# A planner of instruction order gets shared transfer queues, three transfer rates and a replay

## The chip, the cores and the metric

The kernel runs on one core of a Trainium2 chip. The time is device microseconds of one execution, median over runs. Before the change: 1165.82 us, median of 3 runs (1165.45 to 1168.76). The engines are TensorE (PE; its weight loads are listed as PEld), VectorE (DVE), ScalarE (ACT), GpSimd (POOL) and SyncE (SP, which here only issues transfers). Each engine works its own list of instructions strictly in the order in which they were issued; semaphores hold an instruction until its operands are there.

## The reference

A decoder trunk of two layers, 512 tokens, width 1024, float32. Cut to what matters:

```python
for layer in range(2):
    hn = rms_norm(h, attn_norm[layer])
    h = h + (swa_sink_mixer if layer == 0 else nsa_mixer)(hn, ...)
    h = h + swiglu(rms_norm(h, ffn_norm[layer]), w_gu[layer], w_down[layer])   # hidden width 2816
return rms_norm(h, final_norm)
```

Mixer A (layer 0) is attention over a window of 128 with sinks, 16 heads of 64 in 2 key groups. Mixer B (layer 1) adds compressed keys (a two-layer projection of blocks of 32 tokens), selected blocks and a window of 512, mixed by gates. Both have a shared table of relative biases.

## The kernel before

Activations lie transposed, as eight tiles of 128 features by 512 tokens. A float32 product is made of three passes in the format float32r: each operand is cut into a high half (`whi`, `xh`, ...) and the rest (`wlo`, `xl`, ...), and PE multiplies high by high, high by low and low by high.

Stages in order of time: the entry (loads of x, bias tables), the attention of mixer A, its output projection, the feed-forward of layer 0; then the entry of mixer B (key and value projections, compression: tiles `xf`, `xc`, `pc`), its attention, output projection, and the feed-forward of layer 1, which ends in `last_down` and the output.

**The feed-forward** uses `seven`: a product of 2 by 2 blocks in seven block products (`Z`, `X`, `Y` are its PSUM banks) instead of eight. For each of its calls SP loads two raw weight tiles (`raw`, three buffers), DVE makes the sums and differences `s`, ACT casts them to `whi`, DVE subtracts to get `wlo`. For two parts of each call (`wlo` of the first raw tile, and `w22l`) the low half is made by a transfer instead: ACT writes minus the rounded raw tile into it, and a transfer that POOL issues adds the source from HBM onto that, which leaves what the rounding lost (`halves_by_dma`). ACT also evacuates the first two partial sums of `Z` into `rv`, and PE can't start the next product into that bank before. There are 26 calls in each layer: 18 for the gate and up projections, 8 (`seven_down`) for the down projection in two groups of four.

**Buffers.** Most tiles of 128 by 512 come from one ring, `operand` (tag `op`, `NOP` = 38 buffers of 2 KB per partition). In a down stretch 8 of them hold `h`, 21 hold the forms of the hidden layer (7 for each of three blocks, function `hidden_forms`), and a `seven` call takes 4 (`s1`, `s2`, `w22h`, `w22l`), in the gate and up stretches 5 (with `rv`). `scratch` has another 6 (`NT`). `heads_out`, which ends an attention unit, copies half of a bank through a tile `ot` that has two buffers of its own.

**The order of all work** is not that of the source text. Every call of an engine is recorded as an `Op` with a price in ns, the ops that it depends on, and its tiles (class `Scheduler`, `add`); `issue` then lays out a plan and calls the ops in the plan's order. `plan` is a list scheduler: it goes through time, and each free engine takes the ready op with the smallest priority number if its tiles' buffers are free; the port that DVE and POOL share and ACT's table loads are in it. The first priorities come from the longest path to the end and the place in the source (`PLACE`); then `latest` runs the plan backwards and gives each op the latest start as its new priority. Six such rounds (`ROUNDS`) are made and the plan with the shortest own forecast is issued. A transfer in a plan waits for one single line that moves 358 bytes per ns; 1900 ns later it has landed, 1400 ns more for one that POOL issues. All instructions stand under line 119 of the profile, since one helper records them; tiles tell them apart.

Of the kernel before, what the change touches and what calls it, by code (L numbers as in the profile page):

```python
# [16 lines left out]
P = 128  # L17
# [20 lines left out]
RVB = 640  # L38
RVA = 384

NOP = 38
NT = 6
NPT = 2
NW = 3
# [9 lines left out]

PLACE = 300
ROUNDS = 6
DMA_LATENCY = 1900.0

WOK = 6

# [9 lines left out]

class Op:
    __slots__ = ("eng", "call", "cost", "preds", "after", "index", "span", "succs", "prio", "tiles", "table", "bytes", "port", "late")


class Scheduler:
# [46 lines left out]
    def add(self, name, m, call, writes, reads, args, kw):  # L122
        op = Op()
        op.eng, op.call, op.preds, op.succs, op.bytes, op.table, op.late = name, call, {}, [], 0, 0, 0.0
        op.prio = len(self.ops) + self.offset
        n = int(np.prod([c for _, c in writes[0].ap][1:]))
        psum = any("PSUM" in str(x.space) for x in writes + reads)
        parts = writes[0].ap[0][1]

        rows = sum(int(np.prod([c for _, c in x.ap][1:])) > 1 and "PSUM" not in str(x.space) for x in reads)  # L130
        op.port = rows > 0 if name == "pool" else name == "dve" and (
            rows > 1 or rows == 1 and not psum and m in ("tensor_scalar", "tensor_copy"))
        if name == "pe":
            f4 = 1 if m == "transpose" or "float32r" in str(reads[0].dtype) else 4
            op.cost = max(n * f4 * 0.449 + 4.5, 109.0)
        elif m == "dma_start" and name != "pool":
            op.bytes = 4 * int(np.prod([c for _, c in writes[0].ap]))
            op.cost = 475.0 if name == "sp" else 100.0
        elif name == "act":
            extra = sum(isinstance(kw.get(k), bass.AP) for k in ("bias", "scale", "accum_out"))  # L140
            op.cost = n * 0.83 + 93.0 * (1 + extra) - (40.0 if psum else 0.0) + (118.0 if parts == DH else 0.0)
            if m == "activation":
                op.table = self.TABLE.get(args[2].name, 0)
        elif name == "dve":
            if m == "reciprocal":
                op.cost = n * 6.2 + 65.0
            elif m == "memset" or (m in ("tensor_scalar", "tensor_copy") and not psum):
                op.cost = n * 0.52 + 130.0
            else:
                op.cost = n * 1.04 + 70.0 + (60.0 if m == "scalar_tensor_tensor" else 0.0) + (  # L150
                    110.0 if parts < P and n > 100 else 0.0) + (67.0 if m == "tensor_tensor_reduce" else 0.0)
        elif name == "pool":
            if m == "dma_start":

                op.bytes = 8 * int(np.prod([c for _, c in writes[0].ap]))
                op.cost, op.port, op.late = 1000.0, False, 1400.0
            elif m == "tensor_tensor":
                op.cost = n * 2.1 + 150.0
            else:
                op.cost = n * 0.83 + 162.0 + 82.0 * (len(args) > 2 and isinstance(args[2], bass.AP))  # L160
        op.tiles = {}
        for aps, write in ((writes, True), (reads, False)):
            for ap in aps:
                t, box = self.region(ap)
                past = self.seen.setdefault(t, ([], []))
                for w in (0, 1) if write else (0,):
                    for o, q in past[w]:
                        if o is not op and q[0] < box[1] and box[0] < q[1] and q[2] < box[3] and box[2] < q[3]:
                            op.preds[o] = True
                if t in self.tiles:  # L170
                    op.tiles[t] = True
        for aps, w in ((writes, 0), (reads, 1)):
            for ap in aps:
                t, box = self.region(ap)
                self.seen[t][w].append((op, box))
        self.ops.append(op)

    def issue(self):

        ops = self.ops  # L180
        for i, op in enumerate(ops):
            op.index = i
            op.span = op.cost + (op.bytes / 358.0 + DMA_LATENCY + op.late if op.bytes else 0.0)
            op.succs = []
        for op in ops:
            for p in op.preds:
                p.succs.append(op)
        for op in ops:
            op.after = [(q, self.lag(op, q)) for q in op.succs]
        far = {}  # L190
        for op in reversed(ops):
            far[op] = op.span + max((far[q] + (0.0 if q.eng == op.eng else 150.0) for q in op.succs), default=0.0)
        prio = [op.prio * PLACE - far[op] for op in ops]
# [12 lines left out]
    def latest(self, start, span, given):  # L206


        ops = self.ops
        free = {e: 0.0 for e in ("sp", "pe", "act", "dve", "pool")}  # L210
        using = {}
        for op in ops:
            for t in op.tiles:
# [13 lines left out]
        while n:  # L227
# [3 lines left out]
            for e in free:  # L231
# [14 lines left out]
                for p, lag in [(p, self.lag(p, op)) for p in op.preds] + [(p, 150.0) for p in before.get(i, ())]:  # L246
# [6 lines left out]
        return res  # L253

    def plan(self, prio):
        ops = self.ops
# [8 lines left out]
        free = dict(self.tags)  # L265
        first = {tag: 0 for tag in order}
        taken, end_of = set(), {}
        engines = ("sp", "pe", "act", "dve", "pool")
        busy = {e: 0.0 for e in engines}
        port = {"dve": 0.0, "pool": 0.0}  # L270
        ready = {e: [] for e in engines}
        soon = {e: [] for e in engines}
        events, releases = [0.0], []
        waiting = [len(op.preds) for op in ops]
        at = [0.0] * len(ops)
# [4 lines left out]
        table, dma, left, result = 0, 0.0, len(ops), []  # L280
        parked = {tag: [] for tag in order}
        early = {tag: 0 for tag in order}
        finish = 0.0
        freed, given = {tag: [] for tag in order}, {}

        def unpark(tag):
# [4 lines left out]
        def may_take(op):  # L291
# [21 lines left out]
                unpark(tag)  # L313
            return None

        while left:
            assert events, "no instruction can be issued"
            now = heapq.heappop(events)
            while events and events[0] <= now:
                heapq.heappop(events)  # L320
            while releases and releases[0][0] <= now:
                _, tag, t = heapq.heappop(releases)
                free[tag] += 1
                freed[tag].append(t)
                unpark(tag)
            again = True
            while again:
                again = False
                for e in engines:
# [23 lines left out]
                    if op.port:  # L353
                        port[e] = now + cost
                    if op.table and op.table != table:
                        table, cost = op.table, cost + 1280.0
                    start[i] = now
                    busy[e] = end = now + cost
# [3 lines left out]
                    finish = max(finish, end)  # L362
# [3 lines left out]
                    for t in op.tiles:  # L366
                        users[t] -= 1
                        end_of[t] = max(end_of.get(t, 0.0), end)
                        if not users[t]:
                            heapq.heappush(releases, (end_of[t] + 150.0, self.tiles[t], t))  # L370
                            heapq.heappush(events, end_of[t] + 150.0)
                    for q, lag in op.after:
                        k = q.index
                        at[k] = max(at[k], end + lag)
                        waiting[k] -= 1
                        if not waiting[k]:
                            heapq.heappush(soon[q.eng], (at[k], prio[k], k))
                            heapq.heappush(events, at[k])
        return finish, result, start, given


@with_exitstack
def trunk(ctx, tc, a, out):
# [1146 lines left out]
```

## Time and profile before

| | |
|---|---|
| median of 3 runs | 1165.82 us |
| profiled execution | 1163.0 us, its span 1161.2 us |
| granted clock, mean | 0.996 |
| PE busy | 1125.2 us, 97% of the span |
| DVE busy | 905.1 us, 78% |
| ACT busy | 753.4 us, 65% |
| POOL busy | 359.9 us, 31% |
| moved by transfers | 172.02 MB, 148 GB/s over the span |

A busy time is the time in which an engine had at least one instruction under way. "Idle before, releaser" tells how long an engine stood still before an instruction and whose result ended the wait. Transfers have queues: q0 is POOL's, q1 is SP's.

### The profile page before, as it was taken

How to read it: one execution, taken by the hardware profiler on the slowest of the kernel's cores; microseconds unless marked ns; L12 is line 12 of the kernel's file. 1: busy time of each engine (PE TensorE's matmuls, PEld its weight loads, DVE VectorE, ACT ScalarE, POOL GpSimd, SP SyncE). 2: the span in 40 equal slices, each digit the busy share in tenths (PEclk: the TensorE clock that was granted, in tenths of full speed). 3: DMA queues.
4: the chain of work that ended last, by engine and by line, in shares of the span. 5: the costliest groups of instructions: out<-in, count | busy, mean ns of one | idle time of the engine just before them, and what ended most of it. 6: DMA issues, size and time to landing. Idle time of an engine off the chain costs nothing. (4 is left out here: it accounts for less than half of the span.)

```text
span 1161.2 us, 20764 instructions
## 1 busy us (share of the span) xinstructions
PE 1125.2 (97%) x7347; PEld 1005.4 (87%) x7347; DVE 905.1 (78%) x2085; ACT 753.4 (65%) x1557; POOL 359.9 (31%) x519
## 2 busy tenths in 40 slices
PE   8999999999999999999899999999999999999997
PEld 6787787899999998987688788878879999999997
DVE  6999569478878886667788989857857898887764
ACT  5778279367657756552577888829637766775763
POOL 2467711011111121001466867771001121121101
PEclk9999999999999999999899999999999999999999
DMA  7845567477777786861454133156657868778832
GB/s 223 202 96 139 120 150 164 110 189 187 159 184 184 157 189 169 264 199 52 130 124 100 28 92 119 29 125 161 132 121 188 186 155 207 182 166 188 186 96 73
DMA packets 65072, 172.02 MB, mean 148 GB/s; under 512 B 7782, under 2 KB 15718, under 8 KB 64968
## 3 DMA queue, kind: packets, MB, share of 16 engines
q0 software_dynamic: 21312, 58.73, 30.5%
q1 hardware_dynamic: 43376, 111.81, 30.3%
q8 instruction: 58, 0.95, 0.3%
q14 instruction: 46, 0.38, 0.1%
q10 hardware_dynamic: 280, 0.16, 0.1%
HBM read 166.41 MB, written 4.26 MB: 147 GB/s over the span
## 5 line engine op out<-in xcount | busy, mean ns | idle before, releaser
L119 PE MATMUL Z<-xform,whi 128*128 128x256 f32 x864 | 165.0, 284 | 5.8 <-ACT rv L119 5.5
L119 ACT CAST whi<-s 128x512 fp32r<-128x512 f32 (+1 forms) x208 | 115.7, 585 | 76.0 <-PE X L119 47.6
L119 PE MATMUL X<-xform,whi 128*128 128x256 f32 x864 | 164.5, 281 | 0.0
L119 ACT CAST whi<-raw 128x1024 fp32r<-128x1024 f32 (+3 forms) x118 | 107.5, 915 | 71.6 <-PE O L119 27.6
L119 POOL DMA_DIRECT2D wlo<-in_ffn_gu x52 | 45.0, 865 | 339.5 <-ACT wlo L119 207.9
L119 DVE TENSOR_TENSOR wlo<-s,whi 128x512 fp32r<-128x512 f32 (+1 forms) x208 | 129.3, 646 | 17.3 <-ACT whi L119 14.9
L119 PEld LDWEIGHTS Z<-xform,whi 128*128 128x128 f32 x864 | 133.4, 189 | 8.8 <-ACT rv L119 7.0
L119 PEld LDWEIGHTS X<-xform,whi 128*128 128x128 f32 x864 | 135.1, 189 | 0.4
L119 PE MATMUL Z<-xform,wlo 128*128 128x256 f32 x432 | 121.8, 282 | 2.0 <-DMA wlo<-in_ffn_gu 2.0
L119 PE MATMUL X<-xform,wlo 128*128 128x256 f32 x432 | 119.8, 280 | 0.0
L119 DVE TENSOR_TENSOR s<-raw 128x512 f32<-128x512 f32 (+1 forms) x104 | 67.2, 646 | 27.6 <-DMA raw<-in_ffn_gu 22.3
L119 PE MATMUL S<-xh,whi 128*128 128x512 f32 (+1 forms) x216 | 85.7, 408 | 0.6 <-ACT whi L119 0.6
L119 PE MATMUL S<-xl,whi 128*128 128x512 f32 (+1 forms) x216 | 84.6, 405 | 0.0
L119 PEld LDWEIGHTS Z<-xform,wlo 128*128 128x128 f32 x432 | 81.8, 189 | 2.4 <-DMA wlo<-in_ffn_gu 2.4
L119 DVE TENSOR_TENSOR ptl<-PT,pth 128x512 fp32r<-128x512 f32 x108 | 72.5, 686 | 12.0 <-ACT pth L119 10.5
L119 PEld LDWEIGHTS X<-xform,wlo 128*128 128x128 f32 x432 | 81.2, 189 | 0.0
L119 ACT CAST pth<-PT 128x512 fp32r<-128x512 f32 x108 | 61.0, 582 | 30.9 <-PE PT L119 28.9
L119 PE MATMUL S<-xh,wlo 128*128 128x512 f32 x208 | 80.8, 403 | 0.0
L119 ACT ACTIVATE pb<-pb,nmb 128x128 f32<-128x128 f32 (+3 forms) x128 | 71.2, 559 | 9.8 <-DVE nmb L119 9.5
L119 POOL TENSOR_SCALAR pb<-pb,smb,gates 128x128 f32<-128x128 f32 (+3 forms) x120 | 72.1, 614 | 13.5 <-DVE smb L119 10.0
L119 ACT ACTIVATE wlo<-raw 128x1024 fp32r<-128x1024 f32 (+1 forms) x68 | 68.4, 1007 | 0.0
L119 DVE CUSTOM_DVE_ANT_0 pb<-S,bias 128x128 f32<-128x128 f32 (+3 forms) x128 | 59.5, 482 | 4.1 <-PE S L119 3.8
(440 smaller groups left out, 3421.8 us busy)
## 6 DMA issues: line engine op xcount, KB each, us to landing
raw<-in_ffn_gu SPq DMA_DIRECT2D x88, 512.0 KB, 4.5
wlo<-in_ffn_gu POOLq DMA_DIRECT2D x52, 512.0 KB, 6.4
raw<-in_ffn_down SPq DMA_DIRECT2D x48, 384.0 KB, 3.6
w22l<-in_ffn_gu POOLq DMA_DIRECT2D x36, 256.0 KB, 4.7
raw<-in_b_w_in SPq DMA_DIRECT2D x14, 512.0 KB, 3.8
wlo<-in_ffn_down POOLq DMA_DIRECT2D x16, 384.0 KB, 5.0
raw<-in_a_w_qkv SPq DMA_DIRECT2D x9, 512.0 KB, 6.5
h<-in_x SPq DMA_DIRECT2D x16, 256.0 KB, 4.5
```

Source lines behind the costliest of these rows:

```text
L119: self.add(name, m, lambda: getattr(eng, m)(*args, **kw), writes, reads, args, kw)
```

## The change

The arithmetic stays as it is. What changes:

- **Transfers in a plan.** The single line is replaced by a class `Transfers`: a queue for each issuing engine, worked from its head, and all queues that have work share the rate in equal parts. A plain load counts 4 bytes per element, a bias table 14 (was 4), POOL's accumulating transfer 9 (was 8).
- **Rates.** Plans are made for three pairs of rate (bytes per ns) and latency (ns), with six rounds for each, so 18 plans. POOL's transfers land 200 ns sooner than that latency (was 1400 later).
- **Choice.** Each plan's order is replayed, op by op in its order on each engine, with its buffer assignments, under all three pairs; the order with the smallest mean is issued.
- **Prices.** DVE: `tensor_tensor_reduce` +63 only where its scalar is a tensor (was +67 always); `tensor_reduce` by its input's length; `tensor_scalar` with a tensor scalar +80. POOL: +82 for each of up to two tensor scalars (was +82 once).
- **Buffers.** `NOP` 38 to 40; `ot` comes from `scratch` instead of two buffers of its own.

```diff
-NOP = 38
+NOP = 40
-DMA_LATENCY = 1900.0
+SPEEDS = ((390.0, 1650.0), (340.0, 1850.0), (300.0, 2100.0))
+SLOT, TABLE_LOAD = 150.0, 1280.0
...
+class Transfers:
+    def __init__(self):
+        self.coming, self.queues, self.now = [], {e: [] for e in ENGINES}, 0.0
+    def add(self, at, op, alone):
+        heapq.heappush(self.coming, (at, op.index, op, alone))
+    def until(self, now, events):
...
+            active = [q for q in self.queues.values() if q]
+            end = self.now + min(q[0][0] for q in active) * len(active) if active else float("inf")
+            if self.coming and self.coming[0][0] <= min(end, now):
+                at, _, op, alone = heapq.heappop(self.coming)
+                self.pass_to(max(at, self.now), active)
+                self.queues[op.eng].append([alone, op])
+            elif active and end <= now:
+                self.pass_to(end, active)
+                ended += [(q.pop(0)[1], end) for q in active if q[0][0] <= 1e-6]
...
+    def pass_to(self, time, active):
+        for q in active:
+            q[0][0] -= (time - self.now) / len(active)
+        self.now = time
...
         elif m == "dma_start" and name != "pool":
-            op.bytes = 4 * int(np.prod([c for _, c in writes[0].ap]))
+            op.bytes = (14 if writes[0].tensor.name.startswith("bias") else 4) * int(
+                np.prod([c for _, c in writes[0].ap]))
...
+            elif m == "tensor_reduce":
+                op.cost = int(np.prod([c for _, c in reads[0].ap][1:])) * 1.04 + 130.0
             elif m == "memset" or (m in ("tensor_scalar", "tensor_copy") and not psum):
-                op.cost = n * 0.52 + 130.0
+                op.cost = n * 0.52 + 130.0 + 80.0 * (len(args) > 2 and isinstance(args[2], bass.AP))
             else:
                 op.cost = n * 1.04 + 70.0 + (60.0 if m == "scalar_tensor_tensor" else 0.0) + (
-                    110.0 if parts < P and n > 100 else 0.0) + (67.0 if m == "tensor_tensor_reduce" else 0.0)
+                    110.0 if parts < P and n > 100 else 0.0) + (63.0 if isinstance(kw.get("scalar"), bass.AP) else 0.0)
...
-                op.bytes = 8 * int(np.prod([c for _, c in writes[0].ap]))
-                op.cost, op.port, op.late = 1000.0, False, 1400.0
+                op.bytes = 9 * int(np.prod([c for _, c in writes[0].ap]))
+                op.cost, op.port, op.late = 1000.0, False, -200.0
...
-                op.cost = n * 0.83 + 162.0 + 82.0 * (len(args) > 2 and isinstance(args[2], bass.AP))
+                op.cost = n * 0.83 + 162.0 + 82.0 * sum(isinstance(x, bass.AP) for x in args[2:4])
...
         best = None
-        for _ in range(ROUNDS):
-            span, order, start, given = self.plan(prio)
-            if best is None or span < best[0]:
-                best = span, order
-            prio = self.latest(start, span, given)
+        for speed in SPEEDS:
+            self.rate, self.latency = speed
+            for op in ops:
+                op.span = op.cost + (op.bytes / self.rate + self.latency + op.late if op.bytes else 0.0)
...
+            for _ in range(ROUNDS):
+                self.rate, self.latency = speed
+                span, order, start, given = self.plan(prio)
+                prio = self.latest(start, span, given)
+                mean = 0.0
+                for self.rate, self.latency in SPEEDS:
+                    mean += self.replay(order, given) / len(SPEEDS)
+                if best is None or mean < best[0]:
+                    best = mean, order
...
     def plan(self, prio):
...
-                    if op.bytes:
-                        dma = max(dma, end) + op.bytes / 358.0
-                        end = dma + DMA_LATENCY + op.late
+                    if op.bytes:
+                        transfers.add(busy[e], op, op.bytes / self.rate)
+                    else:
+                        complete(op, busy[e])
...
     def heads_out(o, dst, i):
-        t = tile_of("ot", 2, "ot", (DH, T), F32)
+        t = scratch("ot", (DH, T))
```

`replay` (new, not shown) keeps for each engine the plan's list, starts its head as soon as the engine, its inputs, its buffers and the shared port are free, gives transfers to a `Transfers`, and returns the end of the last op. `complete` in `plan` is the old loop over successors and buffers, run when an op or a transfer has ended.

## Rows read from the trace of the kernel before

**Rows 1.** The page, busy time, share of the span and instructions of each engine.

```profile
PE 1125.2 (97%) x7347; PEld 1005.4 (87%) x7347; DVE 905.1 (78%) x2085; ACT 753.4 (65%) x1557; POOL 359.9 (31%) x519
```

**Rows 2.** Windows by stage: from:to, length, then busy us (xinstructions) of each engine, PEclk, DMA, GB/s.

```profile
40.00:122.00 82.00, 77.41 (x428) 62.82 (x426) 77.73 (x258) 61.98 (x192) 55.63 (x82) 1.00 0.55 128
238.00:478.00 240.00, 232.93 (x1937) 229.97 (x1935) 194.25 (x372) 160.04 (x296) 42.60 (x51) 1.00 0.77 177
238.00:306.00 68.00, 68.00 (x571) 67.57 (x570) 56.47 (x106) 49.24 (x93) 11.24 (x13) 1.00 0.75 171
...
534.00:582.00 48.00, 41.97 (x203) 34.17 (x201) 39.17 (x57) 21.39 (x37) 18.32 (x13) 0.93 0.40 111
582.00:766.00 184.00, 181.76 (x1053) 151.07 (x1053) 164.40 (x602) 144.97 (x404) 133.32 (x221) 1.00 0.34 80
860.00:1113.00 253.00, 249.97 (x2050) 246.01 (x2049) 205.18 (x383) 170.43 (x312) 45.04 (x52) 1.00 0.78 180
978.00:1030.00 52.00, 52.00 (x440) 51.82 (x438) 45.60 (x87) 38.88 (x74) 8.68 (x10) 1.00 0.78 176
```

**Rows 3.** Waits of PE, whole span: for whom, us in total, times, longest.

```profile
PE Z L119 <- ACT rv L119: 5.5, 4, 2.6
PE pc L119 <- ACT whi L119: 3.1, 1, 3.1
...
PE Z L119 <- DMA wlo<-in_ffn_gu: 2.0, 2, 1.1
```

**Rows 4.** Timeline of ACT from 370 us: start, us, instruction, idle before and releaser.

```profile
373.81 0.63 ACT L119 ACTIVATE w22l<-raw 128x512 fp32r<-128x512 f32 x1 [2.69 <-DMA raw<-in_ffn_gu]
374.35 0.35 ACT L119 COPY rv<-Z 128x256 f32<-128x256 f32 x1
```

**Rows 5.** Transfers issued from 366.2 to 367.8: xcount, KB, median us to landing.

```profile
raw<-in_ffn_gu SPq DMA_DIRECT2D x2, 512.0 KB, 7.4
wlo<-in_ffn_gu POOLq DMA_DIRECT2D x1, 512.0 KB, 7.2
```

**Rows 6.** Timeline of SP's queue: start, us, issues of raw tiles.

```profile
366.85 0.89 SPq L119 DMA_DIRECT2D raw<-in_ffn_gu  x2
```

**Rows 7.** Transfers of the whole span, by destination and size.

```profile
raw<-in_ffn_gu SPq DMA_DIRECT2D x88, 512.0 KB, 4.5
wlo<-in_ffn_gu POOLq DMA_DIRECT2D x52, 512.0 KB, 6.4
w22l<-in_ffn_gu POOLq DMA_DIRECT2D x36, 256.0 KB, 4.7
...
bias<-rv SPq DMA_DIRECT2D x8, 512.0 KB, 7.8
```

**Rows 8.** POOL by shape: xcount, busy us in all, mean ns, idle before.

```profile
L119 POOL TENSOR_SCALAR pb<-pb,smb,gates 128x512 f32<-128x512 f32 x24 | 19.2, 808 | 7.1 <-DVE smb L119 7.1
...
L119 POOL TENSOR_SCALAR pb<-pb,smb,gates 128x128 f32<-128x128 f32 x32 | 14.0, 446 | 6.1 <-DVE nmb L119 3.4 <-DVE smb L119 2.7
```

**Rows 9.** DVE by shape.

```profile
L119 DVE TENSOR_TENSOR wlo<-s,whi 128x512 fp32r<-128x512 f32 x144 | 95.1, 687 | 15.2 <-ACT whi L119 13.4
...
L119 DVE CUSTOM_DVE_ANT_0 pb<-S,bias 128x512 f32<-128x512 f32 x32 | 21.6, 681 | 0.6 <-PE S L119 0.5
...
L119 DVE TENSOR_TENSOR xf<-ev,pos 64x248 f32<-64x248 f32 x16 | 11.3, 705 | 0.3
```

**Rows 10.** Timeline of ACT in the entry of mixer B.

```profile
553.11 0.70 ACT L119 CAST xc<-xf 128x248 fp32r<-128x248 f32 x2 [4.15 <-DVE xf L119]
```

**Rows 11.** Windows in the entry of mixer B, columns as in Rows 2.

```profile
551.00:555.00 4.00, 0.89 (x7) 0.69 (x6) 3.54 (x8) 1.86 (x4) 0.00 (x0) 0.87 0.46 135
555.00:561.00 6.00, 5.32 (x23) 4.72 (x24) 5.15 (x8) 4.03 (x7) 0.00 (x0) 0.52 0.51 142
```

**Rows 12.** The page, transfer queues: packets, MB, share of the 16 engines' time.

```profile
q0 software_dynamic: 21312, 58.73, 30.5%
q1 hardware_dynamic: 43376, 111.81, 30.3%
```

More of the change, by code (lines that the diff above doesn't have):

```diff
@@ L253, in latest, with replay, complete @@
         return res
+    def replay(self, order, given):
+        ops = self.ops
+        using, after, waiting = {}, [list(op.after) for op in ops], [len(op.preds) for op in ops]
+        for op in ops:
+            for t in op.tiles:
+                using.setdefault(t, []).append(op)
+        for i, ts in given.items():
+            for t in ts:
+                for p in using[t]:
+                    after[p.index].append((i, SLOT))
+                    waiting[i] += 1
+        lines = {e: [op for op in reversed(order) if op.eng == e] for e in ENGINES}
+        busy = {e: 0.0 for e in ENGINES}
+        port = {"dve": 0.0, "pool": 0.0}
+        at, events, finish, table, left = [0.0] * len(ops), [0.0], 0.0, 0, len(ops)
+        transfers = Transfers()
+        def complete(op, end):
+            nonlocal finish
+            finish = max(finish, end)
+            for k, lag in after[op.index]:
+                at[k] = max(at[k], end + lag)
+                waiting[k] -= 1
+                if not waiting[k]:
+                    heapq.heappush(events, at[k])
+        while left:
+            now = heapq.heappop(events)
+            while events and events[0] <= now:
+                heapq.heappop(events)
+            for op, end in transfers.until(now, events):
+                complete(op, end + self.latency + op.late)
+            again = True
+            while again:
+                again = False
+                for e, line in lines.items():
+                    if busy[e] > now or not line:
+                        continue
+                    op = line[-1]
+                    if waiting[op.index] or at[op.index] > now:
+                        continue
+                    other = port["pool" if e == "dve" else "dve"]
+                    if op.port and other > now:
+                        heapq.heappush(events, other)
+                        continue
+                    line.pop()
+                    left -= 1
+                    again, cost = True, op.cost
+                    if op.port:
+                        port[e] = now + cost
+                    if op.table and op.table != table:
+                        table, cost = op.table, cost + TABLE_LOAD
+                    busy[e] = now + cost
+                    heapq.heappush(events, busy[e])
+                    if op.bytes:
+                        transfers.add(busy[e], op, op.bytes / self.rate)
+                    else:
+                        complete(op, busy[e])
+        for op, end in transfers.until(float("inf"), events):
+            complete(op, end + self.latency + op.late)
+        return finish
@@ L320, in plan @@
                 heapq.heappop(events)
+            for op, end in transfers.until(now, events):
+                complete(op, end + self.latency + op.late)
             while releases and releases[0][0] <= now:
@@ L355, in plan @@
                     if op.table and op.table != table:
-                        table, cost = op.table, cost + 1280.0
+                        table, cost = op.table, cost + TABLE_LOAD
                     start[i] = now
-                    busy[e] = end = now + cost
-                    if op.bytes:
-                        dma = max(dma, end) + op.bytes / 358.0
-                        end = dma + DMA_LATENCY + op.late
-                    finish = max(finish, end)
+                    busy[e] = now + cost
                     heapq.heappush(events, busy[e])
@@ L365, in plan @@
                     left -= 1
[L366 to L379, printed above, removed]
+                    if op.bytes:
+                        transfers.add(busy[e], op, op.bytes / self.rate)
+                    else:
+                        complete(op, busy[e])
+        for op, end in transfers.until(float("inf"), events):
+            complete(op, end + self.latency + op.late)
+        return finish[0], result, start, given
 @with_exitstack
```

50 lines of the change are left out of this document (35 added, 15 removed).

## The prediction, written before the changed kernel ran

> **What bounds the kernel now.** I read the busy table first: PE has something under way for 1125.2 us [rows 1] of a span of 1161.2, so 36.0 us are idle, and no other engine is above 78%. The multiplications are not touched, so this change can win from those 36.0 us, or add to them. Next the windows by stage, which tell where the idle time lies (length less PE's busy time) [rows 2]: attention A 82.00 - 77.41 = 4.6; feed-forward of layer 0, 238 to 478, 240.00 - 232.93 = 7.1; entry of mixer B 48.00 - 41.97 = 6.0; attention B 184.00 - 181.76 = 2.2; feed-forward of layer 1, 860 to 1113, 253.00 - 249.97 = 3.0. That is 23.0; the other 13.0 are in the start, the last product and the end, and some between. In each feed-forward there is a stretch without a gap (238 to 306, 978 to 1030) [rows 2], with the same kind of calls as beside it. The limit there is PE; the gaps are places where the order of work failed.
>
> Third, PE's own waits [rows 3]: the largest is for `rv`, 5.5 us in four waits, the longest 2.6. The timeline of ACT shows what that is [rows 4]: ACT stood 2.69 us before a `w22l` instruction whose raw tile had not landed, and the copy of `Z` into `rv`, 0.35 us long, stood behind it in ACT's list. PE could not go on in bank `Z`. So it is a wait in line, made by the order on ACT and by a late raw tile. That tile was one of two issued together from 366.85 [rows 6], beside an accumulating transfer [rows 5].
>
> **The change part by part.** No instruction is added or removed on any engine, no byte moved more or less. Only places in the lists change, and with them who waits. A `seven` call that moves takes along two loads on SP, two transfers on POOL, six casts or copies on ACT and the DVE work between, and passes whatever stood on those four lists; since this can be anywhere, the sum is by stage and not by move. So each part is worth what it does to the 36.0 us.
>
> *Prices of transfers, from issue to landing.* A raw tile of 512 KB was 475 + 524288/358 + 1900 = 3.84 us; now it is 3.47, 3.87 or 4.32 at the three rates if alone; the trace has 4.5 as the median [rows 7]. The accumulating transfer of 512 KB was 1000 + 1048576/358 + 1900 + 1400 = 7.23; now 5.47, 6.12, 6.83; trace 6.4. That of 256 KB was 5.76; now 3.96, 4.38, 4.87; trace 4.7. A bias table was 3.84; now 7.72 at the middle rate; trace 7.8 [rows 7]. So the old prices had raw tiles 0.7 us early and accumulations 0.8 to 1.1 us late. The new middle rate has both 0.3 to 0.6 early when alone, and sharing adds to both. The new prices are nearer, yet a safety margin on the accumulations is gone.
>
> *Prices of instructions.* POOL's scaling of a 128x512 block took 19.2/24 = 0.80 us, of 128x128 14.0/32 = 0.44 [rows 8]; the old prices are 0.67 and 0.35, the new 0.75 and 0.43. DVE's fused minimum on 128x512 shows 681 ns, and an ordinary DVE product of that size, which both planners price at 602, shows 687 [rows 9]: pipelining hides the same 85 ns of each, so 602 is right for both, which is the new price; the old was 669. A price that stays wrong: `xf` in the entry of mixer B, 438 in both planners, 11.3/16 = 0.71 in the trace [rows 9].
>
> *Choice.* 18 plans instead of 6, each judged by replays. This can only pick among plans of the same greedy scheduler.
>
> *Buffers.* In a down stretch 29 of the ring's buffers are held, and 38 leave 9: two calls of 4 and one over. At a change to a gate call (5) they are used up. With 40 the next call can form its `s1` and `s2` while two are in work, which is where gaps lie. The cost is nothing in SBUF, as `ot` gives up two tiles. `ot` now shares six buffers with `ev`, which the query projections take one at a time, so I cost it at nothing; without that cover each of the 32 unit ends would wait for an `ev` to be read, about 0.6 us (a DVE operation of that size [rows 9]), 19 us on ACT, of which PE would see what the two banks of `O` don't bridge.
>
> *The sum, by stage.* (a) Feed-forwards: the two layers do the same work, with 7.1 and 3.0 idle. This shows what the luck of an order is worth, 4.1 in a layer. With nearer prices, two more buffers and more plans I take both at the better level: -4.1. Bounds: all gaps gone, -10.1, as the gapless stretches show possible; both at the worse level, +4.1. (b) Attention A: at the idle share of attention B (2.24 in 184) it would keep 1.0 of 4.6, so -3.6 at best; as much again, +3.6, at worst. DVE is at 77.7 of 82 there [rows 2], so order can do little: I take a third, -1.2. (c) Attention B: 2.2 idle with POOL at 133 of 184; POOL's price was short by about 0.08 on each of some 120 blocks. That is 9.8 us of POOL's time that the old plan did not know, mostly in slack. I take -0.4; bounds -2.2 and +2.2. (d) Entry of mixer B: ACT stood 4.15 us for `xf` [rows 10] with a cast of `whi` behind it, PE waited 3.1 for `whi` [rows 3]. DVE is at 39.2 of 48 and transfers at 0.40 [rows 2], so this is no affair of transfers, and the price of `xf` stays wrong. I take 0. Bounds: gone, -6.0; or doubled, +6.0. [...] (e) Start, last product, end: chains with nothing beside them: 0, within 2.
>
> Sum: -4.1 - 1.2 - 0.4 = **-5.7**. The profiled execution took 1163.0 (span 1161.2 and 1.8 around it) and would become 1157.3. It was 2.8 faster than the median of the runs, 1165.8, and against that I predict **1160.1**.
>
> **A rule weighed against the change.** From 366.85 the first of two raw tiles, issued with an accumulation, released ACT at 373.81: 6.9 us [rows 4, 6]. The new replay, sharing in halves, would say 0.48 + 2 x 1.54 + 1.85 = 5.4 at the middle rate and 6.1 at the lowest. POOL's packets take 0.305 x 1161.2 x 16 / 21312 = 0.27 us of an engine's time, SP's 0.13 [rows 12]. If the two queues took turns packet by packet, POOL's would get two thirds, and the raw tile 0.48 + 3 x 1.54 + 1.85 = 6.9. [...] The trace agrees in this one place. So where the queues meet, every one of the three rates is 0.8 us or more too hopeful on raw tiles. This is the first rival.
>
> **Rivals.** (1) *Shares are unequal, so the gaps stay.* Orders are built on raw tiles that land 0.8 to 1.5 us later than replayed, and ACT and DVE stand in line before `w22l` and `s` as now. For it: the collision above. Against it: the lowest rate is in the mean, and orders that lean on early landings lose there. Then (a) is 0, and -1.6 is left: 1164.2.
>
> (2) *Slower: the lost margin on accumulations.* Plans now place the product that reads `wlo` or `w22l` 0.9 to 1.8 us sooner after its issue than before (7.23 to 5.47 or 6.12; 5.76 to 4.38), and the trace's medians lie 0.3 above the middle price. PE already waits for `wlo` twice, 2.0 us [rows 3], though the old price was 0.8 over the median. The feed-forwards hold 104 of these in 52 calls. If one in six is late by 0.6, PE loses 17 x 0.6 = 10.4; with -1.6 elsewhere: 1174.6. Against it: the replays at 300 see such waits. It decides from about 6 us of waits of `Z`, `X` and `Y` for transfers.
>
> (3) *Nearly all order gaps of the feed-forwards and of attention A go:* -10.1 - 3.6 = -13.7: 1152.1. For it: the gapless stretches. Against it: six rounds of the same method left 10.1.
>
> A new gap like that of (d) at another place costs 3 to 6 us plus the clock, and is the tail of each case.
>
> **How the numbers follow.** The forecast has 0.43, its own range 1156 to 1162; rival 3 has 0.12; rival 1 0.23; rival 2 and other new gaps 0.22. About 0.3%, 3.5 us, is what can be told from no change here (the three runs before span 3.3): under 1162.3 is faster, 0.43 + 0.12 = 0.55; between 1162.3 and 1169.3 is the same, 0.23; above is slower, 0.22. The range goes from 1149 (rival 3 with half of gap (d)) to 1172 (most of rival 2, which with its full price lies outside).
>
> **What would show it.** Right: idle of PE between 27 and 32 us; `Z` waits for `rv` under 3; the windows of both feed-forwards with 2 to 4 idle each. Rival 1: a `w22l` on ACT still waits 2 us and more for its raw tile with a copy into `rv` behind it, and PE's idle time is near 35. Rival 2: PE waits for `wlo` or `w22l` transfers rise above 6. I am wrong about (d) if the entry of mixer B changes by over 3 us, and wrong in the premise if PE's busy time itself changes by more than 3 us apart from the clock.

## The result, and the profile after

The changed kernel takes **1175.92 us** (median of four runs, 1174.68 to 1178.33) against 1165.63 of the kernel before on the same chip: ratio **1.0087**, 95% interval 1.0061 to 1.0113. It is 10.3 us slower, outside the predicted range and on the other side. The two profiled executions are further apart, 15.4 us: that of the kernel before was 2.8 us below its median, that of the changed kernel 2.4 above. The mean granted clock of the first, 0.996, is above that of all 54 other executions of that kernel whose clock is on record (0.985 to 0.995, median 0.991), so the traces overstate what the change costs, by the clock above all.

The busy line of its page and PE's longest waits (for whom, us in total, times, longest):

```profile
span 1176.6 us, 20767 instructions
...
PE 1132.5 (96%) x7347; PEld 1009.2 (86%) x7347; DVE 915.6 (78%) x2085; ACT 749.9 (64%) x1557; POOL 360.4 (31%) x519
```

```profile
PE mm L158 <- DVE h L158: 4.1, 2, 2.9
PE S L158 <- DVE qsa L158: 3.5, 2, 3.0
PE pc L158 <- ACT whi L158: 3.1, 1, 3.1
PE O L158 <- ACT whi L158: 2.8, 1, 2.8
PE Z L158 <- ACT rv L158: 2.5, 1, 2.5
...
PE Z L158 <- DMA wlo<-in_ffn_gu: 1.8, 4, 1.0
```

The first two of these waits, in the kernel before:

```profile
PE mm L119 <- DVE h L119: 2.2, 2, 1.4
...
PE S L119 <- DVE qsa L119: 0.7, 2, 0.4
```

Against [rows 1]: the same 7347, 2085, 1557 and 519 instructions, yet DVE is busy 10.5 us longer, and PE 7.3. PE's idle time is 1176.6 - 1132.5 = 44.1, against 36.0. Against [rows 3]: the waits for `rv` fell from 5.5 to 2.5, as the change means to; the two largest, both for DVE, rose from 2.2 to 4.1 and from 0.7 to 3.5.

The same kinds of window as in [rows 2], each moved to where its stage now stands (length, then busy us of PE, PEld, DVE, ACT, POOL, then PEclk, DMA, GB/s):

```profile
50.00:132.00 82.00, 70.94 (x371) 57.08 (x370) 77.27 (x211) 50.64 (x152) 54.16 (x80) 0.96 0.56 127
248.00:488.00 240.00, 235.49 (x1958) 233.33 (x1957) 195.49 (x375) 161.22 (x298) 42.64 (x53) 0.99 0.79 180
544.00:592.00 48.00, 41.99 (x203) 34.55 (x202) 40.44 (x58) 21.73 (x37) 17.94 (x12) 0.93 0.33 95
592.00:776.00 184.00, 181.37 (x1047) 149.32 (x1046) 163.85 (x603) 143.62 (x403) 131.53 (x218) 1.00 0.35 83
873.00:1126.00 253.00, 249.60 (x2050) 245.58 (x2049) 204.65 (x385) 169.87 (x311) 45.02 (x52) 1.00 0.79 180
```

Attention A has lost: PE stands 11.1 us of 82 in place of 4.6, with a granted clock of 0.96 in place of 1.00. The feed-forward windows stand 4.5 + 3.4 = 7.9 in place of 10.1; the entry of mixer B is as before. Measured between the first products of the four norms (tile `prs`), the stages went: start 29.0 to 25.8, attention A with its output product 144.9 to 157.8, feed-forward of layer 0 355.3 to 357.7, mixer B 278.4 to 279.3, the rest 353.6 to 356.0. The first norm comes 3.2 us earlier, and PE has 732 matmuls in attention A in place of 719. So part of the 12.9 us is work that stood in the start before; up to the second norm it is 174.0 to 183.6, 9.6 us more. DVE is busy for 126.2 us of attention A in place of 115.4, which is all that its busy time rose by.

Why attention A? One DVE instruction, 64x512, usually 0.75 us, shows it. DVE's timeline, then POOL's, at the same time (start, us, engine, operation; `x2` is two instructions in one row, here 5.58 and 0.75):

```profile
79.65 6.36 DVE L158 SCALAR_TENSOR_TENSOR qsa<-ev,bq,qsa 64x512 fp32r<-64x512 f32 x2
```

```profile
79.42 0.85 POOL L158 DMA_DIRECT2D wlo<-in_a_w_qkv  x1
80.06 1.31 POOL L158 TENSOR_SCALAR whi<-raw 128x1024 fp32r<-128x1024 f32 x1
81.08 1.08 POOL L158 TENSOR_SCALAR wlo<-raw 128x768 fp32r<-128x768 f32 x1
81.88 1.07 POOL L158 TENSOR_SCALAR whi<-raw 128x768 fp32r<-128x768 f32 x1
82.66 1.15 POOL L158 DMA_DIRECT2D wlo<-in_a_w_o  x1
83.26 1.42 POOL L158 TENSOR_SCALAR wlo<-raw 128x768 fp32r<-128x768 f32 x1
84.98 0.89 POOL L158 DMA_DIRECT2D wlo<-in_a_w_o  x1 [0.30 <-POOL wlo L158]
```

`qsa` ends at 85.23, 0.55 after the first moment at which POOL pauses (84.68). Note also that from the DMA issue on, each POOL instruction starts 0.2 to 0.55 us before the end of the one ahead. The second case, again DVE, then POOL:

```profile
124.48 4.82 DVE L158 TENSOR_SCALAR pa<-pa,sm 128x256 f32<-128x256 f32 x1
```

```profile
122.38 0.90 POOL L158 DMA_DIRECT2D wlo<-in_a_w_o  x1 [0.30 <-POOL wlo L158]
123.03 4.09 POOL L158 TENSOR_SCALAR pa<-pa,sm 128x128 f32<-128x128 f32 x9
126.85 1.06 POOL L158 TENSOR_SCALAR whi<-raw 128x768 fp32r<-128x768 f32 x1
127.65 1.06 POOL L158 TENSOR_SCALAR wlo<-raw 128x768 fp32r<-128x768 f32 x1
128.46 0.69 POOL L158 TENSOR_SCALAR pa<-pa,sm 128x256 f32<-128x256 f32 x1
```

What it costs PE is in these windows (columns as above): it stands 2.7 and 2.9 us there (the whole gaps are 3.0 and 2.9), and then runs at a granted clock of 0.57 and 0.63 over the next 4 us (0.50 from 85.2 to 88.5 and from 129.6 to 132.8).

```profile
81.00:85.00 4.00, 1.32 (x9) 0.87 (x7) 4.00 (x1) 2.09 (x5) 3.70 (x6) 1.00 0.94 193
85.00:89.00 4.00, 3.72 (x15) 3.38 (x16) 3.89 (x13) 0.43 (x3) 0.87 (x1) 0.57 0.99 240
...
126.00:130.00 4.00, 1.12 (x10) 0.80 (x7) 4.00 (x3) 1.07 (x2) 4.00 (x8) 0.94 0.42 117
130.00:134.00 4.00, 3.98 (x11) 3.19 (x12) 1.16 (x2) 0.00 (x0) 0.54 (x2) 0.63 0.71 123
```

Both planners have one port for DVE and POOL, but let DVE have it as soon as POOL's *running* instruction ends.

### The profile page after: what moved, and what is told of

Its sections match the earlier page's. It is cut to its first block, busy times and chain, and to the rows that moved or that the text cites. A ratio compares the mean times of both kernels' runs of the same rounds, so it can differ in the third digit from the quotient of the medians.

```text
span 1176.6 us, 20767 instructions
## 1 busy us (share of the span) xinstructions
PE 1132.5 (96%) x7347; PEld 1009.2 (86%) x7347; DVE 915.6 (78%) x2085; ACT 749.9 (64%) x1557; POOL 360.4 (31%) x519
## 4 chain that ended last, share of the span: by engine, by line
PE 41%; DVE 4%; DMA 2%; ACT 2%; issue 1%; DVEq 0%; ACTq 0%; SPq 0%; POOLq 0%
PE S L158 8%; PE Z L158 7%; PE O L158 7%; PE X L158 7%; PE mm L158 5%; PE PT L158 3%; PE Y L158 2%; DMA wlo<-in_ffn_gu 1%; DVE pb L158 1%; DVE wlo L158 1%; DVE ptl L158 0%; DVE s L158 0%; ACT xform L158 0%; DVE h L158 0%; DMA raw<-in_ffn_down 0%
```

## The experiments

All times are medians; the chips differ, and the ratios are against the kernel before on the same chip. "DVE excess" is what DVE's instructions took above the 20th percentile of their operation and shape, counted (from 0.15 us up) where one stands beside POOL instructions that overlap as above; attention A is measured between the norms, and beside it stands the time up to the second norm, since the start is shorter in all orders of the changed planner. Each row but those with guards or moved issues is an order of its own, so that the difference between two of them is that of two orders and not the worth of a part alone.

| kernel | us | ratio, 95% interval | attention A | up to the second norm | DVE excess |
|---|---|---|---|---|---|
| before | 1165.6 | 1 | 144.9 | 174.0 | 2.0 |
| changed | 1175.9 | 1.0087, 1.0061 to 1.0113 | 157.8 | 183.6 | 14.7 |
| three guards | 1164.5 | 0.9984, 0.9957 to 1.0012 | 148.8 | 174.9 | 4.1 |
| two DMA issues later | 1166.2 | 1.0002, 0.9985 to 1.0018 | 149.0 | 175.3 | 5.3 |
| guards everywhere | 1166.7 | 1.0009, 0.9989 to 1.0030 | 148.2 | 174.0 | 2.3 |
| before, guards everywhere | 1168.8 | 1.0017, 0.9993 to 1.0041 | 143.5 | 172.0 | 1.2 |
| before, new buffers | 1176.0 | 1.0098, 1.0066 to 1.0130 | 144.5 | 173.8 | 1.0 |
| changed, old buffers | 1175.3 | 1.0096, 1.0062 to 1.0130 | 157.4 | 183.9 | 6.3 |
| changed, old prices | 1185.8 | 1.0185, 1.0151 to 1.0220 | 161.1 | 188.1 | 15.0 |
| changed, one rate | 1203.3 | 1.0318, 1.0276 to 1.0361 | 170.4 | 193.8 | 12.6 |
| rule in the planner | 1169.0 | 1.0020, 0.9997 to 1.0044 | 158.1 | 184.8 | 5.2 |

**Three guards.** POOL waits, ahead of its next port instruction, for the DVE result that had been shut out:

```
 for op in best[1]:
+    if op.index in LET_PASS:              # {743: 535, 1192: 1276, 7339: 7341}
+        self.wait_for(ops[LET_PASS[op.index]].out)   # POOL reads one column of it
     op.call()
```

> The changed kernel in its own order, with three one-column POOL reads added: POOL may start its next whi (twice) or lo copy only after the DVE instruction that in the changed kernel waited out POOL's train (qsa at 79.65 us, 5.58 us long; pa at 124.49, 4.82; pb at 758.01, 2.46). Theory P (DVE is shut out while POOL runs port instructions back to back, and PE then stops and comes back at half clock): these three take under 1 us each, TensorE's gaps at 81.85 (3.2 us), 126.85 (3.1) and 759.7 (1.3) and the half-clock stretches at 85.16 and 129.53 go, the time falls by 6 to 10 us, to 1166 to 1170. Theory M (transfers: the choice for the slowest rate costs) and theory B (buffers) and theory I (instruction prices): the order is unchanged, so the time stays within 2 us of the changed kernel's 1175.9. If DVE's long instructions stay long, port sharing is not what stretches them.

1164.49 us: 11.4 below the changed kernel, a little more than expected. DVE's busy time is 905.0 again. The stretch at 81 to 89 has no gap and no low clock:

```profile
81.00:85.00 4.00, 4.00 (x27) 3.53 (x26) 3.03 (x10) 2.46 (x8) 3.91 (x6) 1.00 0.99 194
85.00:89.00 4.00, 4.00 (x25) 3.40 (x24) 3.74 (x17) 3.95 (x15) 1.76 (x2) 1.00 0.94 195
```

So the loss of the changed kernel is at these places. The third guard took away the gap of 1.2 us at 760.1.

**The parts of the change.** Buffers alone:

```
-NOP = 38
+NOP = 40
-        t = tile_of("ot", 2, "ot", (DH, T), F32)
+        t = scratch("ot", (DH, T))
```

> The kernel before with only the buffers of the change: NOP 40 and the tile ot in the scratch buffers, its own planner otherwise. Theory B (the two more operand buffers and the shared scratch make the planner run POOL and the loads in other places): most of the loss is here, 1171 us or more. Theories M and I: within 3 us of the 1165.6 before. Theory P: the time goes with the number of DVE instructions that wait out a POOL train ahead of TensorE; the sum of DVE's time over nominal was 30 us before and 41 us after, and here the time lies above 1168 only if that sum is above 33.

1176.03: as slow as the whole change. That is a time that theory B gave (1171 or more), but attention A is at 144.5, and the loss stands in the feed-forwards and not at DVE. Its waits:

```profile
PE Z L119 <- ACT rv L119: 13.3, 6, 3.0
PE Z L119 <- DMA wlo<-in_ffn_gu: 3.5, 4, 1.8
```

DVE's time over nominal is 30.4 us, so theory P doesn't explain this loss. The old planner, given 40 buffers, sets six `rv` copies behind late raw tiles in place of four, and the feed-forward of layer 0 takes 365.9 us in place of 355.3. The changed planner with the same buffers has 357.7 and one such wait. The other way round, the changed planner with the old buffers (the same lines taken back):

> The changed planner with the buffers of before (NOP 38, ot in its own two buffers). Theory B: back to 1168 us or less. Theories M and I: 1172 us or more, as the changed kernel. Theory P: the order is another one, so the stretched DVE instructions stand elsewhere; the time lies between 1165 and 1178 and follows their sum (30 us over nominal: about 1166; 41: about 1176).

1175.26, attention A 157.4. Theory B fails here: the buffers are not what costs in the changed order. Theory P's measure fails too: all of DVE's time over nominal is 31.2 us, which said about 1167. PE's longest gap there, 3.0 us from 69.4, stands behind DVE minima in a line and then, for its last 1.3 us, behind a `pa` that waited for one POOL instruction of 1.27 us, not for a train. Old prices (the four lines of the diff with prices of DVE and POOL arithmetic taken back):

> The changed kernel with the old prices of DVE's and POOL's instructions in the planner; the shared transfer rate and the choice over three rates stay. Theory I (the new prices mislead the order): 1169 us or less. Theory M: 1172 or more. Theory P: another order again, 1165 to 1178, with the sum of DVE's time over nominal (30 us: about 1166; 41: about 1176).

1185.77: theory I fails; between these two orders the new prices are worth 10 us. Theory P (1165 to 1178) missed as well, with 42.4 us over nominal. One rate:

```
-SPEEDS = ((390.0, 1650.0), (340.0, 1850.0), (300.0, 2100.0))
+SPEEDS = ((390.0, 1650.0),)
```

> The changed planner with one transfer rate, the fastest (390 B/ns), in place of three: no choice over three rates. Theory M in its form that the choice for the slow rate costs: 1170 us or less, with attention A near the 145 us of before. Theory P (neither planner knows that a POOL train keeps the port): another order, attention A again at 150 us or more or not by chance, the time between 1163 and 1182 and following the sum of DVE's time over nominal in attention A.

1203.27, with six `rv` waits (12.2 us) again: theory M fails, since this order, made for the fast rate alone, is 27 us worse than the one chosen over three. Its queues are shared as well, so sharing alone doesn't keep the `rv` waits away; the three orders chosen over three rates (changed, old buffers, old prices) have one such wait each. The time is outside my range for theory P too: I had not expected the single rate to bring the feed-forward's waits back.

**Guards at every place** where the plan sets a DVE port instruction between two of POOL's, 54 in the changed order and 53 in that of before:

```
+line = sorted((op for op in ops if op.port), key=lambda op: start[op.index])
+let_pass = {b: a for a, b in zip(line, line[1:]) if a.eng == "dve" and b.eng == "pool" ...
+            ... and start[b.index] - start[a.index] - a.cost < LET_PASS}   # 800 ns
```

> The changed kernel in its own order, with the guard at each of the 54 places where its plan puts a VectorE instruction that uses the shared port between two of POOL's, less than 0.8 us before POOL's next: POOL's next waits there for VectorE's result. Theory P: no VectorE instruction stands behind a POOL train of more than one instruction; the sum of DVE's time over nominal falls from 40.7 to below 28 us, attention A to 146 us or less (157.8 changed, 148.8 with three guards), the time to 1158 to 1164. If three guards had taken all that there is, it stays at 1164.5 within 2; if the waits for late VectorE work hold POOL up, whose splits of weights TensorE needs, 1166 to 1172.

> The kernel before in its own order, with the same guards at the 53 places of its own plan. Theory P: it too loses something behind POOL trains (DVE's time over nominal is 30 us, the 2.0 on qsb at 651.7 and the 1.6 on pa at 117.7 with gaps of 1.3 and 1.6 us on TensorE behind them), so it falls by 2 to 5 us, to 1160 to 1163. If the loss is particular to the changed order: within 2 of 1164.4.

1166.72 and 1168.75. All of DVE's time over nominal falls to 25.2 and 25.3 us, but guards also hold POOL up for DVE work that is late: in both, `pc` in the entry of mixer B now waits 4.9 us for `wlo` from POOL. For the changed kernel that is my third case (1166 to 1172). The kernel before gains nothing and misses both of my cases from above: it had only 2.0 us of this to lose, and it got the late `pc` and 9.2 us of waits for `rv` (5.5 before).

**What keeps DVE out, measured by itself.** First, trains of one to six POOL splits with no DMA issue ahead:

```
act.copy(src, other)                                        # start signal
for k in range(train): pool.tensor_scalar(big[k], src, ...)   # 128x1024, 1.0 us each
dve.reciprocal(...) x3; dve.scalar_tensor_tensor(q[64:], ...)  # 64x512
```

> All of the computation is left out; only VectorE and POOL instructions on tiles in SBUF. A POOL train of 1 to 6 tensor_scalar 128x1024 is started, and some 0.3 us later VectorE's scalar_tensor_tensor 64x512 (0.73 us alone) that needs none of their results. Theory P: VectorE's instruction ends behind the whole train, so it takes about 0.7 us + 1.0 for each further POOL instruction (6 of them: 5 to 6 us). The planners' rule (it gets the port after the running POOL instruction): 1.4 us whatever the length. With a wait of POOL for VectorE's result behind the first instruction: 1.4 us. With a DMA issue or a one-column instruction in the train: 1.4 if a pause of POOL hands over the port, as the whole train if not. With a VectorE operand in PSUM: under 1 us.

1.31 or 1.32 us behind trains of every length: **theory P as I had it fell.** The planners' rule is right here, DVE got the port behind the running instruction. With a DMA issue, a one-column instruction or a wait put behind POOL's first instruction it was 1.31 or 1.32 too, as DVE came in ahead of them; with an operand in PSUM it was 0.69. So a train is not enough. In every long case of the changed kernel's attention A, though, the train stands behind a POOL DMA issue and its instructions overlap. That became theory D:

```
steps = [lo, dma] + five splits     against     [lo] + five splits     (and nine scalings)
```

> All of the computation is left out again. VectorE's scalar_tensor_tensor 64x512 starts while POOL runs a train, once with a DMA issue (an accumulation) by POOL in or ahead of the train and once without it; the train is five splits of 128x768 or nine scalings of 128x256 with operands as in attention A. Theory P as it stood (any train keeps the port) has failed: 1.3 us behind one to six instructions. Theory D (behind its own DMA issue POOL starts each next instruction 0.2 to 0.35 us before the end of the one ahead, and as long as it runs so without a pause VectorE doesn't get the port): with the DMA issue VectorE's instruction takes 3 to 5 us, to the end of the train; without it 1.0 to 1.6. A one-column POOL instruction behind the DMA issue changes nothing unless it makes a pause. Rival S (what matters is the kind of instruction, scalings with two per-partition operands, or one more than three in flight): the scalings stretch it with and without the DMA, the splits in neither. If nothing stretches it here, the cause lies in what the whole kernel has beside it (transfers, TensorE and ScalarE at work).

This run missed: the copies meant to delay DVE ran ahead of the start signal, so DVE came during `lo` and took 1.31 to 1.34 us in all 40 cases. It did show the overlap behind each DMA issue (0.35 us, against 0.03 without). With the copies behind the signal:

> The same as the run on trains behind a DMA issue, with VectorE's two to five copies from PSUM put behind the start signal, so that its scalar_tensor_tensor 64x512 arrives in the DMA issue (two), in the first (three) or second (four) instruction behind it; in the run before it came too early, in the instruction ahead of the DMA issue, and took 1.33 us. In that run POOL started each instruction behind the DMA issue 0.35 us before the end of the one ahead, against 0.03 without it. Theory D: with the DMA issue VectorE's instruction takes 3 to 5 us, to the end of the train; without it 1.0 to 1.6; a one-column POOL instruction behind the DMA issue doesn't help. Rival S (the kind of instruction): the nine scalings stretch it with and without the DMA issue, the splits never. If nothing stretches it, what the whole kernel has beside it is needed.

DVE's timeline; the first three rows behind a DMA issue, the last three without it:

```profile
9.85 5.40 DVE L543 SCALAR_TENSOR_TENSOR q<-src,other 64x512 fp32r<-64x512 f32 x1
18.80 4.52 DVE L543 SCALAR_TENSOR_TENSOR q<-src,other 64x512 fp32r<-64x512 f32 x1
27.58 3.78 DVE L543 SCALAR_TENSOR_TENSOR q<-src,other 64x512 fp32r<-64x512 f32 x1
34.18 0.80 DVE L543 SCALAR_TENSOR_TENSOR q<-src,other 64x512 fp32r<-64x512 f32 x1
41.52 0.87 DVE L543 SCALAR_TENSOR_TENSOR q<-src,other 64x512 fp32r<-64x512 f32 x1
48.86 0.94 DVE L543 SCALAR_TENSOR_TENSOR q<-src,other 64x512 fp32r<-64x512 f32 x1
```

The first ends at 15.25, 0.55 behind the last of POOL's five. DVE came in POOL's DMA issue in the first row and in the first split behind it in the second (4.52); the fourth row (0.80) came in the first split of a list that differs only in having no DMA issue. The second round of all cases gave the same within 0.2 us. With a one-column POOL instruction behind the issue DVE took 5.13 and 4.40; with one that waits for a DVE copy, 0.75 both times; POOL paused for 0.40 us in one of these two and not at all in the other, where its instructions behind the waiting one overlap by only 0.03. Nor is it the transfer that holds DVE up: in all 14 long cases DVE ended 0.55 us behind POOL's last instruction, but from 0.13 before to 0.44 behind the landing. The nine scalings with two per-partition operands let DVE in at 0.98, 0.80 and 1.13 even behind the issue: not as expected.

**The same in the kernel, without a wait.** Two of POOL's DMA issues go behind the trains that had followed them:

```
+LATER = ((742, 952), (1044, 1067))
+for a, b in LATER:
+    order.remove(ops[a]); order.insert(order.index(ops[b]), ops[a])
```

> The changed kernel in its own order but for two of POOL's DMA issues in attention A: the one at 79.42 us goes behind the train whi, wlo, whi that followed it (to 82.66), the one at 122.38 behind the train of nine scalings, whi and wlo (to 129.0). No wait is added; POOL's trains are as long and stand at the same place; TensorE uses these weights at 94 and 140 us, so that both transfers still land in time. Theory D (VectorE is shut out only while POOL runs on without a pause behind a DMA issue of its own): qsa at 79.65 takes at most 1.6 us (5.58 changed), pa at 124.49 at most 0.9 (4.82), the gaps at 81.85 and 126.85 and the half-clock stretches behind them go, the time falls by 7 to 11 us to 1165 to 1169. Rival (POOL's trains shut VectorE out there whatever is ahead of them, and the guard helped because it held POOL up): both stay long, the time stays at 1174 to 1178.

1166.20, within the expected 1165 to 1169. POOL's trains are as long as before, but the DMA issue now comes last (POOL, then DVE, whose two `qsa` take 1.38 and 1.20):

```profile
79.97 1.05 POOL L160 TENSOR_SCALAR whi<-raw 128x1024 fp32r<-128x1024 f32 x1
80.99 1.27 POOL L160 TENSOR_SCALAR wlo<-raw 128x768 fp32r<-128x768 f32 x1
82.22 1.27 POOL L160 TENSOR_SCALAR whi<-raw 128x768 fp32r<-128x768 f32 x1
83.44 0.89 POOL L160 DMA_DIRECT2D wlo<-in_a_w_qkv  x1
```

```profile
80.18 2.61 DVE L160 SCALAR_TENSOR_TENSOR qsa<-ev,bq,qsa 64x512 fp32r<-64x512 f32 x2
```

The second place's `pa` takes 0.36. The rival, by which the trains alone shut DVE out, falls: moving two DMA issues takes away 9.7 us.

**The rule in the planner.** Plan and replay let POOL go first from its DMA issue until it pauses:

```
+if e == "pool":
+    chained = op.bytes > 0 or chained and now - busy[e] < 100.0
-for e in ENGINES:
+for e in POOL_FIRST if chained else ENGINES:
```

> The changed kernel with theory D's rule in both its plan and its replay: from a DMA issue of POOL until POOL pauses for 0.1 us, POOL takes the port before VectorE wherever both could start. The order is another one; its replays are 1143.3, 1145.7 and 1154.2 us at the three rates (changed kernel by its own rule: 1137.1, 1140.2, 1150.4). Theory D: no VectorE instruction waits out more than two POOL instructions behind a DMA issue that the plan does not know of; the sum of DVE's time over nominal in such trains is under 5 us (14.7 changed, 2.0 before), attention A is at 150 us or less, and the time is 1160 to 1170. If what the planners miss in attention A is not this, attention A stays at 155 us or more, with the time at 1172 or more.

1168.95, inside the range that theory D gave, but attention A stays at 158.1, on the side of its rival: the gain over the changed kernel is elsewhere, in mixer B (274.2 us between the norms, 278.4 before, 279.3 changed) and behind it (352.7, changed 356.0). The excess is 5.2, just above the bound I set. So this rule is not all that the planner misses in attention A. With the old buffers too it took 157.4 with little shutting out. What costs those two orders their 10 us up to the second norm was not tried. Their traces show the same two signs: PE idle for 7.9 and 8.6 us of attention A, at a mean granted clock of 0.97 and 0.96 (before 4.6 at 1.00, changed 11.1 at 0.98). No version beats the kernel before by more than its interval.

## Why the prediction was wrong

**The step that failed is (b), attention A.** "DVE is at 77.7 of 82 there [rows 2], so order can do little: I take a third, -1.2", with bounds of 3.6 either way. PE's idle time there rose by 6.5 (4.6 to 11.1), and the low clock behind two gaps came on top: two stretches of 3.4 us at a granted clock of 0.50, by estimate 3.4 x 0.5 = 1.7 us lost in each. That is 9.9 us in place of -1.2. I read DVE's 95% as a ceiling on what order could win, and not as a warning: an engine that full, in a stage where POOL is busy 55.6 of 82, has little left to give when it is held up. Two DVE instructions took 4.8 and 4.6 us longer than usual, and PE stood 3.0 and 2.9 us behind them. The guards and the moved issues show that these two make up the 10 us.

**The premise failed at another place than I had named.** "No instruction is added", so I took busy time as fixed and only PE's 36.0 idle us as open. The sign that I gave, PE's busy time changing by more than 3 us apart from the clock, didn't come: it rose by 7.3, and the difference in mean granted clock, 0.996 to 0.989, is worth, by estimate, 0.007 x 1132 = 7.9 (part of that is the high clock of the execution of the kernel before that was profiled). But an instruction shut out counts as busy: DVE's busy time rose by 10.5 with the same count. I never asked whether the *order* changes how long an instruction takes, though both planners carry a term for it, the shared port.

**The tail was priced right and weighed wrong.** I gave a new gap like (d) "3 to 6 us plus the clock" and folded it into the tail of each case; there were two, of 3.0 and 2.9, each with 3.4 us at a granted clock of 0.50. Order that is made afresh everywhere should have had that as a rival with a chance of its own.

**(a) came in its windows and not in its stages.** -4.1 was predicted, and in the windows 10.1 - 7.9 = 2.2 came. The `rv` waits fell to 2.5, under the 3 that I had named as a sign [rows 3]. But the windows leave out the ends of the stages. Between the norms PE stands 7.8 and 6.9 us in the two feed-forwards, against 7.2 and 5.3 before: there (a) is +2.2. The gaps are at other places: at 508.3, behind the window, PE now waits 2.8 for `whi` (waits of `O`), whose cast stands on ACT behind a `sq` that had itself waited 2.49 us for DVE's `h`. With the three guards the windows of [rows 2] stand 3.8 + 1.4 = 5.2, which looks like the whole of (a), yet between the norms it is 7.1 + 4.9 = 12.0 against 12.5. Reading the gain from windows inside the stages was the fault here: a new order moves a gap out of a window as easily as it removes it.

**(c), (d) and (e).** Attention B has 184.00 - 181.37 = 2.6, not 1.8. The entry of mixer B is unchanged, 6.0 idle and PEclk 0.93, as forecast. The start is 3.2 shorter, outside the 2 I allowed, but attention A has taken over its work.

**The rivals.** Rival 2 had the right side by the wrong mechanism: waits of `Z` for `wlo` are 1.8 against 2.0; the margin on accumulations was not needed. (By its own prices "0.9 to 1.8 us sooner" there is 1.1 to 1.8; nothing hangs on it.) Rival 1, unequal shares (that the queues take turns packet by packet was my estimate; it met the 6.9 us of one place [rows 4, 6], and no run tested it), finds one trace: at 291.79 a `w22l` still waits 3.20 us for its raw tile with `rv` behind it, one place of four. Cured of the shut-outs the change is worth nothing that can be measured (0.9957 to 1.0018 over guards and moved issues), where I had 5.7 us, a ratio of 0.9951.

## What to carry to other kernels

Before trusting a new order, look at each DVE instruction's longest time beside its usual one; where it is several times as long (here 5.58 us beside 0.75), look at what POOL does from a DMA issue on, and put the issue at the end of POOL's run of work (9.7 us less here), or a wait behind it (0.75 us in the run by itself). A planner's model of a shared resource must be tested where the new order goes, not only where the old one went: here the transfer model was mended, and the loss came from the port model beside it, whose faults the old order had not met. An engine near its limit in a stage is a reason to widen that stage's range upwards, not to narrow it.

## What the runs showed of the hardware

In the runs by themselves the port went over at the end of POOL's running instruction (1.31 or 1.32 us for DVE's 0.73, behind trains of one to six), except behind a DMA issue of POOL's: there its five splits overlapped by 0.28 to 0.36 us (their starts were 0.80 us apart as without the issue, but each lasted 1.15 us and not 0.83), and DVE waited for the end of the last, up to 5.40 us. Not all DVE work was held up there: in the kernel, behind the issue at 122.38, a 128x4 sum `sm` at 123.95 took 0.29 us (median 0.16), and `pa` half a microsecond later 4.82. In the run by itself the nine scalings with two per-partition operands let DVE in behind the issue (0.80 to 1.13 us), and the first of them waited for DVE (1.02 us, usually 0.54); why these let DVE in stays open.

The length of a gap alone didn't tell whether the clock fell. PE stood 2.6 us shortly ahead of each of these windows, from 372.2 in the kernel before (first row, clock 1.00) and from 290.2 in the changed one (clock 0.60, and 0.50 from 293.4 on):

```profile
374.60:378.00 3.40, 3.24 (x27) 3.24 (x28) 3.38 (x9) 2.54 (x7) 0.86 (x1) 1.00 0.49 70
```

```profile
292.60:296.40 3.80, 3.67 (x19) 3.67 (x20) 3.53 (x8) 3.05 (x7) 0.86 (x1) 0.60 0.48 73
```
